# Decay of a gated linear attention: absolute value moved to ScalarE, the stages of two heads set one unit apart

## The chip, the core and the metric

The program runs on one core of a Trainium2 chip. Times are microseconds (us) of device time of one execution of the whole layer. TensorE (PE) does matmuls, ScalarE (ACT) activations and copies, VectorE (DVE) elementwise work and scans, GpSimd (POOL) further elementwise work; SyncE (SP) issues the transfers. Each engine works through its own instructions in order, and one that waits holds up all behind it.

## The reference

One layer of a decoder with two token mixers. After an RMSNorm, one wide projection of h yields everything: queries, keys and values for both mixers, gates, and a rank-16 code for the decay. The change concerns the decay of the gated linear attention, 4 heads of 128 key channels, 1024 tokens, chunks of 64:

```
log_a = jax.nn.log_sigmoid((g_rank @ w_dec_up + b_dec).astype(jnp.float32)) / GLA_TAU      # GLA_TAU = 16
bcum = jnp.cumsum(la, axis=3)                     # within a chunk
qe = qc * jnp.exp(bcum) * (dk ** -0.5)
ke = kc * jnp.exp(-bcum)
```

log_sigmoid(x) is computed as min(x, 0) - ln(1 + exp(-|x|)).

## The kernel before

Every float32 operand is split into a high and a low part (ScalarE copies the high part, VectorE subtracts it: the helper `split`, L161 to L163), and each product is three matmuls. The projection is cut into jobs of 256 columns. A job is a Strassen-like product of 2 by 2 blocks with seven products, called **units** here and numbered through: unit 0 is the first product of job 0, units 7 and 14 are the first of jobs 1 and 2, unit 21 the first of job 3. A unit is 12 matmuls of 128x512 (L267 to L269).

Which unit touches which bank matters (`unit`, L275 to L298). A job has three PSUM banks, x, y and z. Its units 0, 2, 4 and 6 all accumulate into x: so unit 2 may start only when ScalarE has copied what unit 0 left there (`keep`, L273), unit 4 only after the copy behind unit 2, and unit 6 only when VectorE has read x behind unit 4 (`total`, L306).

The operands of coming units are made ready inside the units before (`Pairs.run`): at a job's unit 0 the split of T3 and T4 of the same job, at its units 2, 4 and 6 the splits of the next job's B11/B21 (from the tile raw), T2/T1 (from tt) and B22 (raw to dh, dl). tt holds four differences that GpSimd forms from raw (L241 to L244), for one job at a time: GpSimd starts on the next job when T3 and T4 are split. `run(1, mid)` issues the splits, then the list `mid`, then the unit with its eviction.

The decay of the 4 heads is laid into the first 20 units by such lists, heads 0 and 1 first, then 2 and 3, since the tiles U and E have two buffers each. For head h:

- `logit` (L774): two matmuls (L778) into two banks of the tag tr, of which there are two; VectorE adds the bias from each bank into U (L779).
- `decay_a` (L783): VectorE, E = min(-U, U). `decay_b` (L786): ScalarE, E = exp(E). `decay_c` (L789): ScalarE, E = ln(E + 1).
- `decay_d` (L792): VectorE, E = min(U, 0) - E. `decay_e` (L795): VectorE, the scan along the tokens, into U.
- `decay_f` (L798, L799): ScalarE, E = exp(U/16) and U = exp(-U/16). `decay_g` (L802 to L804): VectorE copies 16 columns out of E; SyncE stores E and U.

The instructions of ScalarE and VectorE stand in these units in the order of the program; PE's are ordered by the scheduler. The chains of heads 2 and 3 are the end of the stage: their last instructions stand in units 16 to 19.

Of the kernel before, what the change touches and what calls it, by code (L numbers as in the profile page):

```python
# [11 lines left out]
AF = mybir.ActivationFunctionType  # L12
ALU = mybir.AluOpType
# [40 lines left out]
class Line:  # L54
# [5 lines left out]
    def run(self, n=None):  # L60
        while self.items and (n is None or n > 0 or not self.items[0][1]):
            f, unit = self.items.pop(0)
            f()
            if unit and n is not None:
                n -= 1


class Pairs:
# [7 lines left out]
        self.at = 0  # L76
        self.first = [j["load"] for j in self.jobs[:2]] + self.jobs[0]["split"][:3]

    def run(self, n=None, mid=()):
        while self.at < 7 * len(self.jobs) and (n is None or n > 0):  # L80
            i, u = divmod(self.at, 7)
            nxt = self.jobs[i + 1] if i + 1 < len(self.jobs) else None
            if u == 0:
                self.jobs[i]["split"][3]()
            elif nxt and u in (2, 4, 6):
                nxt["split"][u // 2 - 1]()
            if u == 1 and i + 2 < len(self.jobs):
                self.jobs[i + 2]["load"]()
            for fn, arg in mid:
                fn(arg)  # L90
            due = self.late.pop(0) if self.late else None
            self.jobs[i]["unit"](u)
            if due:
                due()
            self.at += 1
            if n is not None:
                n -= 1
# [3 lines left out]
def hybrid_layer(ctx: ExitStack, tc: tile.TileContext, x, norm_g, w_in, w_up, b_dec,  # L101
# [5 lines left out]
    nc = tc.nc  # L107
# [421 lines left out]
    def qk_pair(c0, i, dst):  # L529
        def evict(J, n, bank, add):  # L530
            v = total(bank, add)
            o = stage()
            split(v, o[:, 0], o[:, 1])
            nc.sync.dma_start(dst[2 * i + J][:, :, half(n)], o.bitcast(F32))

        return pair_job(w_in, c0 + i * DV, evict)
# [23 lines left out]
    def gg_pair(h):  # L560
        return pair_job(w_in, C_GG + h * DV,
                        lambda J, n, bank, add: silu(total(bank, add), d_gg[h][:, J, half(n)]))

    def merge_pair(c0, i, dst):
        def evict(J, n, bank, add):
            if add is None:
                add = ev.tile([P, HALF], F32, tag="f", name="f")
                nc.scalar.activation(add, bank, AF.Copy)
            else:
                total(bank, add)  # L570
            nc.sync.dma_start(dst[2 * i + J][:, half(n)], add)

        return pair_job(w_in, c0 + i * DV, evict)
# [6 lines left out]
    def sg_pair(i):  # L580

        return pair_job(w_in, C_SG + i * DV,
                        lambda J, n, bank, add: silu(total(bank, add), d_sg[2 * i + J][:, half(n)]))

    def sv_pair(i):


        held = []

        def evict(J, n, bank, add):  # L590
            if add is None:
                add = ev.tile([P, HALF], F32, tag="f", name="f")
                nc.scalar.activation(add, bank, AF.Copy)
            else:
                total(bank, add)
            h = 2 * i + J
            nc.vector.tensor_copy(vend[:, h, 4 * n:4 * n + 4], add[:, P - 1:HALF:P])
            held.append((J, n, h, add))
            if (J, n) != (1, 1):
                while held:  # L600
                    diff(*held.pop())

        def diff(J, n, h, add):
            d = ev.tile([P, HALF], F32, tag="f", name="f")
            nc.vector.tensor_sub(d[:, 1:HALF], add[:, 0:HALF - 1], add[:, 1:HALF])
            if n:
                nc.vector.tensor_sub(d[:, 0:1], vend[:, h, 3:4], add[:, 0:1])
            else:
                nc.vector.tensor_scalar(d[:, 0:1], add[:, 0:1], -1.0, None, op0=ALU.mult)

            def turn():
                pt = ps.tile([P, HALF], F32, tag="tr", name="tr")
                for b in range(4):
                    nc.tensor.transpose(pt[:, b * P:(b + 1) * P], d[:, b * P:(b + 1) * P], ident)
                o = stage()
                split(pt, o[:, 0], o[:, 1])
                for e in range(2):
                    nc.sync.dma_start(d_v[h][:, 4 * n:4 * n + 4, e],
                                      o[:, e].bitcast(F32).rearrange("p (b c) -> p b c", c=P))

            late.append(turn)

        return pair_job(w_in, C_SV + i * DV, evict)

    def gla_qk(i):
        return [gqk_pair(C_GQ, i, inv_sqrt, d_e1, d_gq), gqk_pair(C_GK, i, 1.0, d_e2, d_gk)]

    late = []
    pairs = Pairs([merge_pair(C_MA, i, d_ga) for i in range(3)] +
                  gla_qk(0) + [gg_pair(0), gg_pair(1)] + gla_qk(1) + [gg_pair(2), gg_pair(3)] +  # L630
                  [f for i in range(4) for f in (qk_pair(C_SQ, i, d_q), qk_pair(C_SK, i, d_k))] +
                  [sg_pair(i) for i in range(3)] + [merge_pair(C_MB, i, d_gb) for i in range(4)] +
                  [sv_pair(i) for i in range(4)] + [merge_pair(C_MA, 3, d_ga)], late)
# [132 lines left out]
    U, E = {}, {}  # L766
# [13 lines left out]


    def decay_a(h):
        nc.vector.scalar_tensor_tensor(E[h], U[h], -1.0, U[h], op0=ALU.mult, op1=ALU.min)  # L783

    def decay_b(h):
        nc.scalar.activation(E[h], E[h], AF.Exp)  # L786

    def decay_c(h):
        nc.scalar.activation(E[h], E[h], AF.Ln, bias=1.0)  # L789
# [13 lines left out]
        nc.sync.dma_start(d_e1[h], E[h])  # L803
        nc.sync.dma_start(d_e2[h], U[h])  # L804

    djobs = [[(code, 0)], [(code, 1)]]
    for h in (0, 2):
        djobs += [[(logit, h)], [(logit, h + 1), (decay_a, h)], [(decay_b, h), (decay_a, h + 1)],
                  [(decay_b, h + 1), (decay_c, h)], [(decay_c, h + 1), (decay_d, h), (decay_e, h)],
                  [(decay_d, h + 1), (decay_e, h + 1)], [(decay_f, h)], [(decay_f, h + 1), (decay_g, h)], [(decay_g, h + 1)]]  # L810
    manual = ExitStack()
    manual.enter_context(tc.manual_schedule(engines={mybir.EngineType.Activation, mybir.EngineType.DVE}))
    for jobs in djobs:
        pairs.run(1, jobs)
    dq_ctx.close()


# [22 lines left out]

    tjobs = [[] for _ in range(GLA_AT - len(djobs))]
    for k in range(8):
        at = 4 * k + 3
        for i in range(2):
            tjobs[at + i].append((t_load, (k, i)))
            tjobs[at + 9 + i].append((t_store, (k, i)))
        for i in range(4):
            tjobs[at + 6 + i // 2].append((t_sum, (k, i)))
# [739 lines left out]
```

## Time and profile before

| | before |
|---|---|
| median of 3 runs | 1182.15 us (1180.53 to 1182.76) |
| the profiled execution | 1181.14 us |
| its span, first to last instruction | 1179.4 us |
| PE busy | 1163.8 us, 99% of the span |
| VectorE, ScalarE, GpSimd busy | 861.1, 554.1, 248.2 us |
| decay in the span | from 102.6 us (its first transposes) to 163.1 us (last exponential) |

In a row of a timeline the first number is the start in the span, the second how long the instruction took, then engine, line, operation, output <- inputs, and the shape; x2 means that two in a row are shown as one; in brackets stands how long the engine had been idle before and what ended that.

### The profile page before, as it was taken

The page shows a single profiled execution, that of the slowest core. Times are in us where ns is not written, and L with a number is a line of the kernel's source. Part 1 is how long each engine was busy: PE and PEld are TensorE (multiplying, and loading weights), DVE is VectorE, ACT ScalarE, POOL GpSimd, SP SyncE. Part 2 cuts the span into 40 slices and gives each one's busy share as a digit, 9 for nine tenths or more (in the row PEclk, how much of TensorE's full clock was granted, in tenths as well). Part 3 has the DMA queues.
Part 4 walks back from the last instruction along what each step waited for, and adds up shares of the span by engine and source line. Part 5 has one row for each costly group of instructions (what it writes and reads, how often), then busy time and mean ns, then how long its engine had stood idle before and what let it go on. Part 6 is the DMA issues. An engine that isn't in the chain of part 4 may idle for free.

```text
span 1179.4 us, 16601 instructions
## 1 busy us (share of the span) xinstructions
PE 1163.8 (99%) x5811; PEld 978.4 (83%) x5811; DVE 861.1 (73%) x1440; ACT 554.1 (47%) x1040; POOL 248.2 (21%) x217
## 2 busy tenths in 40 slices
PE   8999999999999999999999999999999999999997
PEld 8999778888888888888888888888888888888886
DVE  6797866887676876776666677457777876588986
ACT  6555652433545544545444343344454544364543
POOL 1022341324242242342242232000000000700001
PEclk9999999999999999999999999999999999999999
DMA  7325469897355565654444357799756556858652
GB/s 289 126 63 161 173 233 320 294 308 242 123 189 185 186 221 165 196 179 136 154 144 132 109 173 240 258 310 333 258 188 226 194 166 196 281 162 286 212 197 107
DMA packets 189455, 239.23 MB, mean 203 GB/s; under 512 B 12438, under 2 KB 128172, under 8 KB 187836
## 3 DMA queue, kind: packets, MB, share of 16 engines
q1 hardware_dynamic: 188796, 237.13, 60.9%
q8 instruction: 45, 0.74, 0.3%
q10 hardware_dynamic: 576, 1.05, 0.2%
q14 instruction: 38, 0.31, 0.1%
HBM read 150.06 MB, written 88.08 MB: 202 GB/s over the span
## 4 chain that ended last, share of the span: by engine, by line
PE 89%; DVE 4%; ACT 2%; issue 2%; DMA 2%; POOL 1%; SPq 0%; ACTq 0%; DVEq 0%
PE pp L267 16%; PE pp L269 16%; PE pp L268 16%; PE pp L203 3%; PE pp L202 3%; PE pp L201 3%; PE pp L220 2%; PE tr L1083 1%; PE av L1106 1%; PE av L1105 1%; PE av L1104 1%; PE z L1065 1%; PE z L1067 1%; PE z L1066 1%; PE xb L1472 1%
## 5 line engine op out<-in xcount | busy, mean ns | idle before, releaser
L267 PE MATMUL pp<-S,wh 128*128 128x512 f32 x372 | 147.2, 396 | 1.0 <-ACT f L273 1.0
L269 PE MATMUL pp<-S,wl 128*128 128x512 f32 x372 | 145.0, 390 | 0.0
L268 PE MATMUL pp<-S,wh 128*128 128x512 f32 x372 | 145.0, 390 | 0.0
L306 DVE TENSOR_TENSOR f<-pp,f 128x512 f32<-128x512 f32 x93 | 63.9, 687 | 76.0 <-PE pp L269 65.0
L163 DVE TENSOR_TENSOR wl<-tt,wh 128x1024 fp32r<-128x1024 f32 x62 | 75.9, 1224 | 51.5 <-ACT wh L162 51.1
L162 ACT ACTIVATE wh<-tt 128x1024 fp32r<-128x1024 f32 x62 | 65.7, 1059 | 74.8 <-PE pp L268 67.3
L241 POOL TENSOR_TENSOR tt<-raw 128x512 f32<-128x512 f32 x31 | 44.4, 1432 | 258.3 <-DVE wl L163 250.5
L273 ACT ACTIVATE f<-pp 128x512 f32<-128x512 f32 x93 | 54.9, 592 | 88.1 <-PE pp L269 84.8
L1071 DVE TENSOR_TENSOR_SCAN be<-be,m 128x128 f32<-128x128 f32 (+3 forms) x64 | 86.1, 1348 | 6.9 <-ACT be L1068 6.7
L162 ACT ACTIVATE wh<-raw 128x1024 fp32r<-128x1024 f32 (+1 forms) x47 | 48.4, 1031 | 85.9 <-PE pp L268 51.5
L267 PEld LDWEIGHTS pp<-S,wh 128*128 128x128 f32 x372 | 70.5, 190 | 15.9 <-ACT f L273 1.8
L269 PEld LDWEIGHTS pp<-S,wl 128*128 128x128 f32 x372 | 69.8, 188 | 14.9
L268 PEld LDWEIGHTS pp<-S,wh 128*128 128x128 f32 x372 | 69.9, 188 | 13.7
L163 DVE TENSOR_TENSOR wl<-raw,wh 128x1024 fp32r<-128x1024 f32 (+1 forms) x47 | 63.8, 1357 | 15.8 <-ACT wh L162 15.2
L228 POOL TENSOR_TENSOR r<-r,nhalf 128x1 f32<-128x1 f32 x40 | 25.2, 629 | 194.5 <-DVE r L227 194.5
L1068 ACT ACTIVATE be<-z 128x384 f32<-128x384 f32 (+4 forms) x96 | 47.2, 495 | 22.5 <-PE z L1067 20.0
L1255 POOL TENSOR_TENSOR N<-A,A 128x512 f32<-128x512 f32 x4 | 5.7, 1424 | 242.1 <-DMA A<-d_osb 242.1
L267 PE MATMUL pp<-ha22h,wh 128*128 128x512 f32 x124 | 48.8, 394 | 0.7 <-DVE f L306 0.7
L267 PE MATMUL pp<-ha11h,wh 128*128 128x512 f32 x124 | 49.2, 397 | 0.0
L267 PE MATMUL pp<-ha12h,wh 128*128 128x512 f32 x124 | 49.1, 396 | 0.0
L267 PE MATMUL pp<-S,dh 128*128 128x512 f32 x124 | 48.6, 392 | 0.0
L244 POOL TENSOR_TENSOR tt<-raw,tt 128x512 f32<-128x512 f32 x31 | 48.0, 1549 | 2.2
(528 smaller groups left out, 3398.4 us busy)
## 6 DMA issues: line engine op xcount, KB each, us to landing
raw<-in_w_in_dram SPq DMA_DIRECT2D x31, 1024.0 KB, 5.8
d_t<-t SPq DMA_DIRECT2D x16, 512.0 KB, 6.6
d_ogl<-o SPq DMA_DIRECT2D x64, 128.0 KB, 2.5
d_q<-o SPq DMA_DIRECT2D x16, 512.0 KB, 3.2
d_k<-o SPq DMA_DIRECT2D x16, 512.0 KB, 4.8
d_v<-o SPq DMA_DIRECT2D x32, 256.0 KB, 2.3
k<-d_k SPq DMA_DIRECT2D x8, 1024.0 KB, 6.1
v<-d_v SPq DMA_DIRECT2D x16, 512.0 KB, 5.1
```

What stands on the lines that cost most here:

```text
L162: nc.scalar.activation(hi, src, AF.Copy)
L163: eng.tensor_sub(lo, src, hi.bitcast(F32))
L201: nc.tensor.matmul(pt, whi[:, kb], h_, start=kb == 0, stop=False)
L241: nc.gpsimd.tensor_sub(t1, b[:, 0, 1], b[:, 0, 0])
L244: nc.gpsimd.tensor_sub(t4, b[:, 1, 0], t2)
L267: nc.tensor.matmul(pt, bh[:, j], ah[:, j], start=first and j == 0, stop=False, skip_group_check=True)
L268: nc.tensor.matmul(pt, bh[:, j], al[:, j], start=False, stop=False, skip_group_check=True)
L269: nc.tensor.matmul(pt, bl[:, j], ah[:, j], start=False, stop=j == 3, skip_group_check=True)
L273: nc.scalar.activation(t[nm], t[bank], AF.Copy)
L306: nc.vector.tensor_add(add, bank, add)
L1068: nc.scalar.activation(om[:, off + pc * w:off + (pc + 1) * w], zt[:, 0:w], AF.Sigmoid, scale=-inv_sqrt)
L1071: nc.vector.tensor_tensor_scan(rest, rest, m1[:, off:T][:, ::-1], 1.0, op0=ALU.mult, op1=ALU.max)
```

## The change

`decay_a` becomes an activation Abs on ScalarE, and `decay_b` gets the factor -1. `Pairs.run` gets a second list, `post`, that is issued behind the unit and its eviction; `decay_f` goes there. Of the two heads of a pair, the second now has its scan (`decay_e`) one unit behind its `decay_d`. Heads 2 and 3 begin at unit 10 in place of 11, so that the decay takes 19 units and not 20; the lists that follow are shifted by one entry to stay at the same units.

```
-    def run(self, n=None, mid=()):
+    def run(self, n=None, mid=(), post=()):
...
             self.jobs[i]["unit"](u)
+            for fn, arg in post:
+                fn(arg)
...
     def decay_a(h):
-        nc.vector.scalar_tensor_tensor(E[h], U[h], -1.0, U[h], op0=ALU.mult, op1=ALU.min)
+        nc.scalar.activation(E[h], U[h], AF.Abs)
 
     def decay_b(h):
-        nc.scalar.activation(E[h], E[h], AF.Exp)
+        nc.scalar.activation(E[h], E[h], AF.Exp, scale=-1.0)
...
-    djobs = [[(code, 0)], [(code, 1)]]
-    for h in (0, 2):
-        djobs += [[(logit, h)], [(logit, h + 1), (decay_a, h)], [(decay_b, h), (decay_a, h + 1)],
-                  [(decay_b, h + 1), (decay_c, h)], [(decay_c, h + 1), (decay_d, h), (decay_e, h)],
-                  [(decay_d, h + 1), (decay_e, h + 1)], [(decay_f, h)], [(decay_f, h + 1), (decay_g, h)], [(decay_g, h + 1)]]
+    djobs = [([(code, 0)], []), ([(code, 1)], [])] + [([], []) for _ in range(17)]
+    for h, at in ((0, 2), (2, 10)):
+        for i, fn, h_ in ((0, logit, h), (1, logit, h + 1), (1, decay_a, h), (2, decay_b, h), (2, decay_a, h + 1),
+                          (3, decay_b, h + 1), (3, decay_c, h), (4, decay_c, h + 1), (4, decay_d, h), (4, decay_e, h),
+                          (5, decay_d, h + 1), (6, decay_e, h + 1), (7, decay_g, h), (8, decay_g, h + 1)):
+            djobs[at + i][0].append((fn, h_))
+        for i, h_ in ((6, h), (7, h + 1)):
+            djobs[at + i][1].append((decay_f, h_))
...
-        pairs.run(1, jobs)
+        pairs.run(1, *jobs)
...
-        at = 4 * k + 3
+        at = 4 * k + 4
```

Line numbers after the change are two higher up to the decay, and a few more behind it (L162 is L164, L273 is L275, L778 is L780, L786 is L788, L789 is L791, L798 and L799 are L800 and L801).

Three places show what this moves. The first is PE where the logits of head 3 are computed. Before, its two matmuls stand inside unit 12 (the products with dh and dl; S_1004 and S_1005 are the high and low part of S4), with three others between them:

```order
L269 MATMUL pp<-S_1080,wl 128x512
L267 MATMUL pp<-S_1004,dh 128x512
L268 MATMUL pp<-S_1005,dh 128x512
L778 MATMUL tr<-rst,o 128x512
L269 MATMUL pp<-S_1004,dl 128x512
L267 MATMUL pp<-S_1004,dh 128x512
L268 MATMUL pp<-S_1005,dh 128x512
L778 MATMUL tr<-rst,o 128x512
```

Now both stand together between unit 10 (with S_807 and S_808, the parts of S1) and unit 11 (S_1080 and S_1081, of S3):

```order
L269 MATMUL pp<-S_807,wh 128x512
L270 MATMUL pp<-S_808,wh 128x512
L271 MATMUL pp<-S_807,wl 128x512
L780 MATMUL tr<-rst,o 128x512 x2
L269 MATMUL pp<-S_1080,wh 128x512
L270 MATMUL pp<-S_1081,wh 128x512
```

Head 2's pair stands in front of unit 10, where before it stood in front of unit 11: between it and the first matmul of head 3 lay 14 matmuls, and now lie 12. On VectorE head 2's two bias additions now follow directly on the copies of head 1's `decay_g`, where a split of tt stood between.

The second place is ScalarE around unit 13, in heads 2 and 3. Before, from the split of B22 (dh) on: one exponential, the eviction of unit 13 (L568), the split of T3 and T4 (wh from tt), the other exponential, a table load, the logarithms:

```order
L162 ACTIVATE dh<-raw 128x512
L786 ACTIVATE e<-e 128x1024
L568 ACTIVATE f<-pp 128x512
L162 ACTIVATE wh<-tt 128x1024
L786 ACTIVATE e<-e 128x1024
L789 ACT_TABLE_LOAD
L789 ACTIVATE e<-e 128x1024
L273 ACTIVATE f<-pp 128x512
```

Now the exponential, the table load and the first logarithm stand ahead of that eviction and that split:

```order
L164 ACTIVATE dh<-raw 128x512
L788 ACTIVATE e<-e 128x1024
L791 ACT_TABLE_LOAD
L791 ACTIVATE e<-e 128x1024
L570 ACTIVATE f<-pp 128x512
L164 ACTIVATE wh<-tt 128x1024
L791 ACTIVATE e<-e 128x1024
L275 ACTIVATE f<-pp 128x512
```

The third place is ScalarE around units 17 and 18. Before, from the last table load: head 2's two exponentials, the copy behind unit 17, the split of tt for unit 18 (T2 and T1 of job 3), then head 3's two exponentials:

```order
L798 ACT_TABLE_LOAD
L798 ACTIVATE e<-u 128x1024
L799 ACTIVATE u<-u 128x1024
L273 ACTIVATE f<-pp 128x512
L162 ACTIVATE wh<-tt 128x1024
L798 ACTIVATE e<-u 128x1024
L799 ACTIVATE u<-u 128x1024
L162 ACTIVATE dh<-raw 128x512
```

Now head 3's exponentials, as the list behind unit 17, stand ahead of that split:

```order
L800 ACT_TABLE_LOAD
L800 ACTIVATE e<-u 128x1024
L801 ACTIVATE u<-u 128x1024
L275 ACTIVATE f<-pp 128x512
L800 ACTIVATE e<-u 128x1024
L801 ACTIVATE u<-u 128x1024
L164 ACTIVATE wh<-tt 128x1024
L164 ACTIVATE dh<-raw 128x512
```

On VectorE the lower part of that split is followed, before and now, by one small copy of `decay_g` (head 2's before, head 3's now) and then by the reading of bank x behind unit 18. The number of table loads in the stage is four in both. Behind the decay no engine's order changes.

## The prediction

> **What bounds the kernel now.** I read the page's head first, then the waits of PE in the stretch of the decay (102 to 166 us), then the timelines of PE, VectorE, ScalarE and GpSimd there.
>
> ```profile
> span 1179.4 us, 16601 instructions
> PE 1163.8 (99%) x5811; PEld 978.4 (83%) x5811; DVE 861.1 (73%) x1440; ACT 554.1 (47%) x1040; POOL 248.2 (21%) x217
> PE pp L267 <- ACT f L273: 1.0, 1, 1.0
> PE pp L267 <- DVE f L306: 0.7, 1, 0.7
> PE tr L778 <- DVE u L779: 0.3, 1, 0.3
> ```
>
> PE is busy 99% of the span, so the end moves only by what PE waits. An engine with time to spare gains nothing from less work; it counts only where PE waits for it. In the decay these are three waits, 2.0 us together. Their exact size, with a fourth, is in PE's timeline: each row before a wait, and the row behind it.
>
> ```profile
> 134.36 0.61 PE L778 MATMUL tr<-rst,o 128*128 128x512 f32 x2
> 135.97 0.50 PE L267 MATMUL pp<-S,wh 128*128 128x512 f32 x1 [1.00 <-ACT f L273]
> 139.05 0.39 PE L268 MATMUL pp<-S,dh 128*128 128x512 f32 x1
> 139.73 0.50 PE L778 MATMUL tr<-rst,o 128*128 128x512 f32 x1 [0.29 <-DVE u L779]
> 150.53 0.39 PE L269 MATMUL pp<-ha12h,wl 128*128 128x512 f32 x1
> 150.91 0.50 PE L267 MATMUL pp<-S,wh 128*128 128x512 f32 x1
> 161.70 0.39 PE L269 MATMUL pp<-S,dl 128*128 128x512 f32 x1
> 162.80 0.50 PE L267 MATMUL pp<-ha22h,wh 128*128 128x512 f32 x1 [0.72 <-DVE f L306]
> ```
>
> A matmul starts every 0.227 us (the two at 134.36 take 0.61 together, one alone 0.39). So unit 11 should have started at 134.81 and came at 135.97, 1.16 late; the logit of head 3 came 0.45 late, unit 16 0.15, unit 20 0.87. Each first matmul after a wait takes 0.50 in place of 0.39, 0.11 more. Sum: 2.63 + 0.44 = 3.07 us, 0.26% of the time. That is all the change can win, unless it makes the rest of the program quicker, and behind the decay the order is the same.
>
> **The parts that cost nothing by themselves.** VectorE loses four L783 (1.2 us each), ScalarE gets four Abs. Abs isn't in this trace. The nearest row is an activation of the same shape:
>
> ```profile
> 119.49 1.06 ACT L786 ACTIVATE e<-e 128x1024 f32<-128x1024 f32 x1 [1.48 <-DVE e L783]
> ```
>
> I take its 1.06, with 0.60 (half the shape, the eviction at 145.51 below) and 1.3 (a table load, at 148.02 below) as ends. The order shows the same four table loads, so none is added. PE waits for no Abs directly. The exponential of head 1 waited 1.48 here for VectorE's L783; now Abs takes 1.06 of ScalarE in that place, so the chain of heads 0 and 1 comes some 0.4 earlier. The factor -1 in the exponential changes no shape. The stores of E and U keep their places in SyncE's queue, but for the very last one, which now goes ahead of one store of gate logits; the next to need them is unit 21. I set all this at 0, ends -0.4 and +0.5.
>
> **Head 3's logits now wait for VectorE (+0.9).** VectorE and GpSimd in the stretch where heads 0 and 1 end:
>
> ```profile
> 129.98 3.27 DVE L795 TENSOR_TENSOR_SCAN u<-rmask,e 128x1024 f32<-128x1024 f32 x1
> 133.17 0.66 DVE L306 TENSOR_TENSOR f<-pp,f 128x512 f32<-128x512 f32 x1
> 133.76 1.68 DVE L163 TENSOR_TENSOR wl<-raw,wh 128x1024 fp32r<-128x1024 f32 x1
> 135.35 1.32 DVE L802 COPY ebl<-e 128x16 f32<-128x16 f32 x2
> 138.94 1.40 DVE L779 TENSOR_SCALAR u<-tr,vcol 128x512 f32<-128x512 f32 x2
> 131.06 3.28 POOL L243 TENSOR_TENSOR tt<-raw 128x512 f32<-128x512 f32 x1
> 134.31 2.25 POOL L242 TENSOR_TENSOR tt<-raw,tt 128x512 f32<-128x512 f32 x1
> 136.64 1.30 POOL L244 TENSOR_TENSOR tt<-raw,tt 128x512 f32<-128x512 f32 x1
> ```
>
> See how they exclude each other. The scan takes 3.27, where 2.29 is its time alone (a row below). GpSimd's L243 takes 3.28, where L244 at 136.64 takes 1.30: it waits for the scan's end at 133.25. The split at 133.76 takes 1.68 and not 1.23: it waits for L243's end at 134.34. The copies of heads 0 and 1 start at 135.35 and end at 136.67, just behind L242 (136.56). Only the work on PSUM (L306, L779) goes on beside. I call this the lock. Up to these copies VectorE's order is unchanged, so they end at about 136.4 (the 0.4 from above, less a little). Then head 2's bias additions follow: 0.7 each, to 137.1 and 137.8.
>
> PE is there earlier. Unit 10 began at 134.36 less its 12 x 0.227, at 131.64. Now head 2's two matmuls and unit 10 stand there, 14 x 0.227, so head 3's first matmul is due at 134.82. It needs the first tr bank, free at 137.1: 2.3 late, and the second 0.26 more. With the slow restart 2.7 us, where before the first two waits cost 1.16 + 0.11 + 0.45 + 0.11 = 1.83. The wait of unit 11 for ScalarE's copy goes, since that copy now stands ahead of head 1's exponentials; but it is replaced by a longer one. Net +0.9. The wait at unit 16 goes (-0.26): PE comes there 1 us later, and the copy it needs does not.
>
> **Unit 20 now waits behind head 3's exponentials (+4.4).** ScalarE and VectorE at the end of the decay:
>
> ```profile
> 142.57 0.63 ACT L162 ACTIVATE dh<-raw 128x512 fp32r<-128x512 f32 x1 [4.91 <-PE pp L268]
> 145.51 0.60 ACT L568 ACTIVATE f<-pp 128x512 f32<-128x512 f32 x1 [1.03 <-PE pp L269]
> 146.01 1.05 ACT L162 ACTIVATE wh<-tt 128x1024 fp32r<-128x1024 f32 x1
> 148.02 1.28 ACT L789 ACT_TABLE_LOAD   x1
> 158.41 1.05 ACT L162 ACTIVATE wh<-tt 128x1024 fp32r<-128x1024 f32 x1
> 160.98 1.06 ACT L798 ACTIVATE e<-u 128x1024 f32<-128x1024 f32 x1 [1.52 <-DVE u L795]
> 147.09 1.23 DVE L163 TENSOR_TENSOR wl<-tt,wh 128x1024 fp32r<-128x1024 f32 x1 [1.37 <-ACT wh L162]
> 150.41 1.61 DVE L792 SCALAR_TENSOR_TENSOR e<-u,e 128x1024 f32<-128x1024 f32 x1 [2.09 <-ACT e L789]
> 152.05 3.27 DVE L795 TENSOR_TENSOR_SCAN u<-rmask,e 128x1024 f32<-128x1024 f32 x1
> 155.82 1.67 DVE L163 TENSOR_TENSOR wl<-raw,wh 128x1024 fp32r<-128x1024 f32 x1
> 158.66 2.29 DVE L795 TENSOR_TENSOR_SCAN u<-rmask,e 128x1024 f32<-128x1024 f32 x1
> 162.07 0.68 DVE L306 TENSOR_TENSOR f<-pp,f 128x512 f32<-128x512 f32 x1
> ```
>
> Unit 20 needs the reading of bank x at 162.07. In VectorE's queue that stands behind the split whose upper part is ScalarE's row at 158.41. That row came before head 3's exponentials (160.98, which waited for the scan). Now it comes behind both. Step by step, from unit 11: it starts 2.7 us behind 134.82 + 0.45, at 138.0, and two units of 2.72 bring unit 13 to 143.5:
>
> - dh can start when unit 12 is done, 143.7. Then 0.49 for it, 0.96 exponential, 1.29 table load, 0.96 logarithm, 0.49 eviction, 0.96 split (rows that follow each other lie 0.1 closer than they last): the split of T3 and T4 is done at 149.0, on VectorE at 150.15, where it was at 148.3.
> - From there to the end of the second scan VectorE has 1.13 (L792) + 2.2 (scan) + 1.13 (L792) + 1.13 (split) + 2.2 (scan) = 7.8 under the lock, and GpSimd, which starts behind the same split, its four differences of 1.2. Before, two of these four ran while VectorE waited for the logarithm (150.41); now there is no such gap, and they alternate. Sum 12.6, end at 162.8. Before, it was 160.95.
> - Head 3's exponentials 2.2, the split 1.06, its lower part 1.2, a copy 0.1, the reading 0.7, with the signals between: 168.1.
> - PE: unit 13 at 143.5, seven units of 2.72 and one matmul that is drawn ahead: due at 162.8. So it waits 5.3, and 0.11 for the restart, where 0.98 stood: +4.4.
>
> What else would hold PE in that gap? Nothing is queued for it: the rest of the order is behind this unit.
>
> **The clock after such a gap (+2.4).** After the waits in the rows above, of 1.2 us or less, only the first matmul was slow. Longer stretches without PE are only at the two ends:
>
> ```profile
> 1.42 5.91 PE L146 MATMUL warm<-ident 128*128 128x128 f32 x26 [1.42 <-POOL ident masks.py:199]
> 8.52 1.06 PE L146 MATMUL warm<-ident 128*128 128x128 f32 x8
> 1172.50:1174.50 2.00, 0.00 (x0) 0.00 (x0) 1.56 (x3) 1.26 (x3) 0.21 (x1) 1.00 0.43 165
> 1174.50:1175.00 0.50, 0.00 (x0) 0.00 (x0) 0.13 (x1) 0.08 (x2) 0.34 (x1) 0.90 0.55 217
> 1175.00:1179.40 4.40, 0.00 (x0) 0.00 (x0) 0.62 (x1) 0.71 (x1) 0.00 (x0) 0.50 0.56 214
> ```
>
> After the last matmul the granted clock (the column ahead of the last two) falls to 0.50 within 2.4 us. At the start the same 128x128 matmul takes 5.91 / 26 = 0.23 us each, and from 8.52 on 0.13: PE ran slow for some 6 to 7 us of steady work. So a gap of 5.3 us should end with the clock at half, and PE should need between half of that time and all of it to come back: 3.3 to 6.6 us at half speed, 1.6 to 3.3 lost. I take 2.4, with 0 (no drop) as the other end. [...]
>
> **Sum.** 0.9 - 0.26 + 4.4 + 2.4 = +7.4. Against the profiled execution (1181.14, of which 1.7 lie outside the span) that is 1188.5; the median of the three runs is 1.0 higher than this execution, which would give 1189.5. I say 1189.0.
>
> **The rivals.**
> - *The clock stays up.* The same waits, no slow stretch: 1181.6 (between the two bases) + 5.0 = 1186.6. Against it stands the tail; for it, that the tail is one case, and that PE's clock is seen to fall nowhere else. [...]
> - *The lock does not bite.* Were GpSimd's differences out of the way, the copies would end at 133.5 and both tr banks be free by 134.9: no wait there. The second scan would end at 155.9, unit 20 be due at 160.0 and have its bank at 161.4: 1.5 + 0.11 in place of 3.07, 1180.1. Against it: the stretched rows above; GpSimd starts on the same splits as before.
> - *The change does what its parts say, and the waits go: faster.* For it: the copy for unit 11 does stand ahead of the exponentials now, and heads 2 and 3 begin a unit earlier. If VectorE had head 2's additions done by 134.8 and head 3's scan ended at 157.6, 5.2 us ahead of what I say, all four waits would go: 3.07 less, 1178.5. That is the point that decides; the scan ended at 160.95 before, and the work ahead of it has only moved together.
> - *The second wait is milder.* If GpSimd loses two turns to VectorE, the scan ends 2.4 earlier and no clock falls: +2.6, 1184.2.
> - *Both gaps cool PE.* The first, 2.6 us in all, is near the tail's 2.4: another 1.6 to 2.4, 1191.
>
> **Chances and range.** Forecast 0.56; clock stays 0.17; lock does not bite 0.08; waits go 0.07; milder 0.07; both gaps 0.05. A measurement of this kernel can tell about 0.2% from no change, 2.4 us: faster is below 1179.8, slower above 1184.5. Faster: the case of the waits and a little of the lock's, 0.08. Same: the rest of the lock's and a small part of the milder, 0.09. Slower 0.83. The range from 1183.5 to 1192.0 leaves out the waits' and the lock's case and a little above.
>
> **What will show it.** In the profile after: PE's waits in the decay are two: the second logit pair (L780) for VectorE's L781, 2 to 2.6 us, at about 135; and unit 20 (ha22h) for VectorE's L308, 4.5 to 5.5 us, at about 163. The wait for ScalarE's copy (L275) is gone. ScalarE's split of tt follows head 3's exponentials directly. Behind 168 the granted clock shows a slow stretch of 3 to 7 us. I am wrong if unit 20 waits under 2 us, if the second scan ends ahead of 160, or if PE waits somewhere else for longer.

## The result and the profile after

The kernel after takes 1188.01 us (median of 6 runs, 1185.47 to 1188.6), before 1180.83 (6 runs, 1179.89 to 1182.76): ratio 1.0054, 95% interval 1.0044 to 1.0065. It is slower by some 7 us; the forecast was 1189.0. The profiled execution took 1187.92 us with a span of 1186.2, 6.8 more than before.

PE's waits from 102 to 175 us, to set beside the three waits of before:

```profile
PE pp L269 <- DVE f L308: 4.5, 1, 4.5
PE tr L780 <- DVE u L781: 2.1, 2, 1.9
```

The wait for ScalarE's copy is gone. The two waits for VectorE, 0.7 and 0.3 before, have grown, at the two places that the prediction named. The timeline of PE has the rows around both:

```profile
134.62 0.39 PE L271 MATMUL pp<-S,wl 128*128 128x512 f32 x1
136.92 0.50 PE L780 MATMUL tr<-rst,o 128*128 128x512 f32 x1 [1.91 <-DVE u L781]
137.57 0.50 PE L780 MATMUL tr<-rst,o 128*128 128x512 f32 x1 [0.15 <-DVE u L781]
...
164.04 0.39 PE L269 MATMUL pp<-ha11h,wh 128*128 128x512 f32 x1
168.89 0.80 PE L269 MATMUL pp<-ha22h,wh 128*128 128x512 f32 x1 [4.46 <-DVE f L308]
...
169.91 0.63 PE L271 MATMUL pp<-ha22h,wl 128*128 128x512 f32 x1
170.33 0.63 PE L269 MATMUL pp<-ha22h,wh 128*128 128x512 f32 x1
```

Head 3's logits came 2.07 and 0.42 us late (136.92 less 134.62 + 0.227, and so on), unit 20 came 4.62 late. The last two rows show a matmul every 0.42 us in place of 0.227; it was so behind both gaps. The windows there show why. A row gives a stretch and its length, then the busy time of PE, of its weight loads, of VectorE, ScalarE and GpSimd with their instructions in brackets; the granted clock is the column ahead of the last two:

```profile
134.70:138.10 3.40, 1.33 (x5) 0.67 (x4) 3.40 (x6) 2.48 (x4) 2.67 (x2) 1.00 0.81 330
138.20:141.40 3.20, 3.20 (x9) 2.53 (x8) 1.77 (x3) 2.53 (x3) 0.00 (x0) 0.50 0.00 0
165.40:168.80 3.40, 0.00 (x0) 0.00 (x0) 1.88 (x4) 2.01 (x3) 0.00 (x0) 1.00 0.75 308
169.00:172.20 3.20, 3.20 (x8) 2.52 (x9) 1.03 (x2) 0.00 (x0) 0.00 (x0) 0.50 0.69 205
```

The granted clock fell to half behind both gaps, not only behind the second. The slow matmuls lost 1.56 us at the first (8 times 0.195) and 1.65 at the second. Summed over the stretch, PE is 10.4 us late where it was 3.07 late before: +7.4, against +6.8 in the span. The other 0.6 comes back far behind the decay: a transpose at 706.84 us of before starts 7.40 later in after, one at 914.67 only 6.86 later, as before waits 0.47 and 0.67 for VectorE between 912 and 915 us and after, there, 0.52 once.

The causes stand in the other engines' timelines. VectorE and GpSimd, with the rows of the prediction's steps:

```profile
133.29 1.67 DVE L165 TENSOR_TENSOR wl<-raw,wh 128x1024 fp32r<-128x1024 f32 x1
134.89 1.31 DVE L804 COPY ebl<-e 128x16 f32<-128x16 f32 x2
136.12 1.39 DVE L781 TENSOR_SCALAR u<-tr,vcol 128x512 f32<-128x512 f32 x2
150.39 1.22 DVE L165 TENSOR_TENSOR wl<-tt,wh 128x1024 fp32r<-128x1024 f32 x1 [3.90 <-ACT wh L164]
152.79 3.27 DVE L797 TENSOR_TENSOR_SCAN u<-rmask,e 128x1024 f32<-128x1024 f32 x1
155.98 2.24 DVE L794 SCALAR_TENSOR_TENSOR e<-u,e 128x1024 f32<-128x1024 f32 x1
158.75 1.72 DVE L165 TENSOR_TENSOR wl<-raw,wh 128x1024 fp32r<-128x1024 f32 x1
160.39 3.37 DVE L797 TENSOR_TENSOR_SCAN u<-rmask,e 128x1024 f32<-128x1024 f32 x1
166.92 1.23 DVE L165 TENSOR_TENSOR wl<-tt,wh 128x1024 fp32r<-128x1024 f32 x1 [3.09 <-ACT wh L164]
168.15 1.28 DVE L308 TENSOR_TENSOR f<-pp,f 128x512 f32<-128x512 f32 x2
133.84 2.25 POOL L244 TENSOR_TENSOR tt<-raw,tt 128x512 f32<-128x512 f32 x1
153.87 3.27 POOL L245 TENSOR_TENSOR tt<-raw 128x512 f32<-128x512 f32 x1
159.46 2.16 POOL L246 TENSOR_TENSOR tt<-raw,tt 128x512 f32<-128x512 f32 x1
```

At 134.89 the two copies of 16 columns take 1.31 together, to 136.20, just behind GpSimd's L244 (133.84 to 136.09); only then come head 2's additions. From 150.39 on, VectorE and GpSimd alternate: scans of 3.27 and 3.37, an L794 of 2.24, until 163.76. ScalarE:

```profile
144.97 0.63 ACT L164 ACTIVATE dh<-raw 128x512 fp32r<-128x512 f32 x1 [3.91 <-PE pp L270]
163.79 1.06 ACT L800 ACTIVATE e<-u 128x1024 f32<-128x1024 f32 x1 [3.17 <-DVE u L797]
164.88 1.06 ACT L801 ACTIVATE u<-u 128x1024 f32<-128x1024 f32 x1
165.85 1.04 ACT L164 ACTIVATE wh<-tt 128x1024 fp32r<-128x1024 f32 x1
```

The split at 165.85 stands behind head 3's two exponentials; VectorE's lower part (166.92), its reading of bank x (168.15) and unit 20 (168.89) follow one upon the other.

### The profile page after: what moved, and what is told of

It is laid out like the page before. It is cut to its first block, busy times and chain, and to the rows that moved or that the text cites. A ratio compares the mean times of both kernels' runs of the same rounds, so it can differ in the third digit from the quotient of the medians.

```text
span 1186.2 us, 16600 instructions
## 1 busy us (share of the span) xinstructions
PE 1165.6 (98%) x5811; PEld 979.9 (83%) x5811; DVE 857.4 (72%) x1436; ACT 558.6 (47%) x1044; POOL 250.2 (21%) x217
## 4 chain that ended last, share of the span: by engine, by line
PE 88%; DVE 4%; DMA 3%; ACT 2%; issue 2%; SPq 0%; ACTq 0%; DVEq 0%
PE pp L269 16%; PE pp L270 16%; PE pp L271 16%; PE pp L204 3%; PE pp L203 3%; PE pp L205 3%; PE pp L222 2%; PE av L1111 1%; PE av L1110 1%; PE av L1109 1%; PE tr L1088 1%; PE xb L1477 1%; PE xb L1475 1%; PE xb L1476 1%; PE z L1070 1%
## 5 line engine op out<-in xcount | busy, mean ns | idle before, releaser
L164 ACT ACTIVATE wh<-tt 128x1024 fp32r<-128x1024 f32 x62 | 65.6, 1058 | 75.1 <-PE pp L270 67.3
L275 ACT ACTIVATE f<-pp 128x512 f32<-128x512 f32 x93 | 55.1, 593 | 87.8 <-PE pp L271 80.4
L164 ACT ACTIVATE wh<-raw 128x1024 fp32r<-128x1024 f32 (+1 forms) x47 | 48.5, 1031 | 86.2 <-PE pp L270 50.9
L270 PE MATMUL pp<-ha22l,wh 128*128 128x512 f32 x124 | 48.9, 394 | 0.0
L271 PE MATMUL pp<-ha22h,wl 128*128 128x512 f32 x124 | 48.8, 394 | 0.0
```

The source lines that it names most:

```text
L164: nc.scalar.activation(hi, src, AF.Copy)
L270: nc.tensor.matmul(pt, bh[:, j], al[:, j], start=False, stop=False, skip_group_check=True)
L271: nc.tensor.matmul(pt, bl[:, j], ah[:, j], start=False, stop=j == 3, skip_group_check=True)
L275: nc.scalar.activation(t[nm], t[bank], AF.Copy)
```

## The experiments

All were timed in five rounds beside before, whose median was 1180.77 to 1181.22 us in each set. The theory: two gaps and the clock behind each are the whole loss; the first comes from the lock on the copies, the second from head 3's exponentials ahead of the split, with the lock on the way to them. The rivals: Abs costs; the spread costs wherever it stands; the lock is no cause; the slow stretches do not come from the gaps.

**Abs alone.** Before, with two lines changed:

```
-        nc.vector.scalar_tensor_tensor(E[h], U[h], -1.0, U[h], op0=ALU.mult, op1=ALU.min)
+        nc.scalar.activation(E[h], U[h], AF.Abs)
...
-        nc.scalar.activation(E[h], E[h], AF.Exp)
+        nc.scalar.activation(E[h], E[h], AF.Exp, scale=-1.0)
```

> The kernel before with only the absolute value on ScalarE (Abs, then exp with the factor -1); order of the stages as before. My theory, that Abs itself costs nothing and the loss lies in where the stages stand: the time of before, -0.5 to +0.3 us, the wait of unit 11 a little shorter than 1.16, the wait of unit 20 about 0.9 as before, no slow clock. Rival, that four more activations on ScalarE are what delays the copies and splits: +1 us or more, with PE waits on ScalarE's rows.

1180.15 us, ratio 0.9995 (0.9986 to 1.0003). The rows of an Abs and of unit 11's first matmul:

```profile
139.88 1.06 ACT L783 ACTIVATE e<-u 128x1024 f32<-128x1024 f32 x1 [2.72 <-DVE u L779]
135.48 0.50 PE L267 MATMUL pp<-S,wh 128*128 128x512 f32 x1 [0.52 <-ACT f L273]
```

An Abs takes 1.06. Unit 11 came 0.68 late in place of 1.16. The Abs costs nothing.

**The spread alone.** After, with these lines put back as in before (the minimum on VectorE).

> The changed kernel with the absolute value back on VectorE, all else as changed. Theory (the order of the stages is the loss): as slow as the changed kernel, +6.5 to +8 us over before, both waits there (logits of head 3 about 2 to 2.6, unit 20 about 4.5 to 5.5) and the clock at half behind each. Rival (Abs is the loss): within 2 us of before.

1189.65 us, ratio 1.0071 (1.0058 to 1.0084): both waits (2.56 and 0.43 late, 4.63 late), both slow stretches. The order makes the loss.

**Head 3's exponentials behind the split.** After, with one of the four pairs placed elsewhere:

```
-            djobs[at + i][1].append((decay_f, h_))
+            if h_ == 3:
+                djobs[18][0].insert(0, (decay_f, h_))
+            else:
+                djobs[at + i][1].append((decay_f, h_))
```

> The changed kernel with head 3's two exponentials moved behind the split of T2 and T1 at unit 18, where they stood before; nothing else is moved. Theory (unit 20 waits because that split stands behind them): the split is done before the second scan ends, the wait of unit 20 falls from 4.5 to about 1 to 2.4, and with it the slow clock behind it; the wait for head 3's logits (about 2) and the slow clock behind it stay. Time +2.5 to +4 over before. Rival (the second scan itself, late by GpSimd's lock, holds the reading of bank x): the wait stays over 4 and the time at +6 or more.

1183.65 us, ratio 1.0021 (1.0012 to 1.0029). PE's timeline has one row that matters, against 4.46 in after:

```profile
167.13 0.50 PE L269 MATMUL pp<-ha22h,wh 128*128 128x512 f32 x1 [1.52 <-DVE f L308]
```

Unit 20 waits 1.52, and behind it the matmuls come at full pace (the next at 167.48). The first gap and its slow stretch are as in after. So the place of head 3's exponentials was worth 4.4 of the 7 us.

**Without GpSimd's differences of job 3.** After, where tt is only set to a constant for that job, so that the kernel leaves out a part of the result:

```
+            if not sums:
+                nc.gpsimd.memset(tt, 0.5)
+                t["b"], t["tt"] = b, tt
+                return
...
-        return pair_job(w_in, c0 + i * DV, evict, before)
+        return pair_job(w_in, c0 + i * DV, evict, before, sums=(c0, i) != (C_GQ, 0))
```

> After without GpSimd's four differences for job 3: a memset of tt stands in their place, so that job's part of the projection (the gated attention's queries of heads 0 and 1) is not computed from the input. Theory (GpSimd and VectorE exclude each other; the differences stretch VectorE's way to head 3's scan): L794, scan, L794, split, scan run at their own lengths, the second scan ends near 159.5 in place of 163.7, and unit 20 waits about 1.7 us in place of 4.6 and its clock stays up behind it; the first gap behind head 3's logits is unchanged (the differences of job 2 stand there). Time about 1.1 + 1.6 us above before, some 1183.5. Rival (the scan is late because of ScalarE's order, the lock is no cause): unit 20 waits over 4 us as in after, time as after.

1183.4 us, ratio 1.002 (1.0011 to 1.0029). VectorE's and GpSimd's timelines, to set beside the rows from 150 on above (the line numbers of the decay are four higher here):

```profile
152.69 2.29 DVE L801 TENSOR_TENSOR_SCAN u<-rmask,e 128x1024 f32<-128x1024 f32 x1
154.89 1.20 DVE L798 SCALAR_TENSOR_TENSOR e<-u,e 128x1024 f32<-128x1024 f32 x1
156.61 1.22 DVE L165 TENSOR_TENSOR wl<-raw,wh 128x1024 fp32r<-128x1024 f32 x1
157.74 2.29 DVE L801 TENSOR_TENSOR_SCAN u<-rmask,e 128x1024 f32<-128x1024 f32 x1
151.57 1.81 POOL L244 MEMSET tt<- 128x2048 f32 x1 [14.21 <-DVE wl L165]
```

All instructions have their own lengths, the second scan ends at 160.0 and not 163.8, and unit 20 comes 1.33 late in place of 4.62, with the clock up. ScalarE's order is that of after. So the second wait has two causes that make it long only together, the lock and the place of head 3's exponentials: with either one taken away it is under 2 us.

**Spare matmuls in the gap.** After, with work for PE ahead of unit 20 that nothing reads:

```
+        if pairs.at == 20:
+            fill = ps.tile([P, HALF], F32, tag="av", name="fill", bufs=1)
+            for _ in range(16):
+                nc.tensor.matmul(fill, ident, kept_f[C_MA, 2, 0, 0], start=True, stop=True)
```

> The changed kernel with 16 more matmuls of 128x512 into an unused bank ahead of unit 20 (they read a tile that has long been written, and nothing reads the bank). They take 16 x 0.227 = 3.6 us of a gap of 4.6. Theory (the gap lets the clock fall, which costs 1.6 us in slow matmuls): unit 20 starts at the same time, its matmuls come every 0.227 and not 0.43, and the time is 1.3 to 1.7 us below the changed kernel. Rival (the slow matmuls behind the gap have another cause, such as operands or banks): they stay slow and the time is that of the changed kernel or more.

1196.97 us, ratio 1.014 (1.0126 to 1.0155). The expectation was wrong by the price of a matmul: on float32 operands one took 0.83 us, not 0.227 (16 from 164.04 to 177.38), and they overshot the gap by 8.5 us. With five in place of sixteen (the profile shows each as two rows):

> After with five spare matmuls of 128x512 (float32, identity times the value tile, into a bank of their own that nothing reads) ahead of unit 20. In the run with sixteen they took about 0.83 us each, so five take some 4.2 us of the 4.85 us in which PE stands there otherwise. Theory (the gap itself cools PE, by 1.6 us): unit 20 starts at the time it starts in after (168.9), behind it the matmuls come every 0.23 us and not 0.43, and the kernel takes 1.3 to 1.7 us less than after, about 1186.5. Rival (the slow stretch belongs to the units behind, or to the time of the run, not to the gap): the stretch stays and the time is that of after, or longer by what the spare matmuls overshoot.

1186.71 us (1186.2 to 1186.99), ratio 1.005 (1.0037 to 1.0062). PE's timeline:

```profile
163.93 4.46 PE L862 MATMUL fill<-f,ident 128*128 128x512 f32 x10
168.76 0.50 PE L269 MATMUL pp<-ha22h,wh 128*128 128x512 f32 x1 [0.37 <-DVE f L308]
169.09 0.39 PE L270 MATMUL pp<-ha22l,wh 128*128 128x512 f32 x1
```

Unit 20 starts at the same time as in after (168.89), but no slow stretch follows. The median lies 1.3 us below after's, the size expected. The intervals of the two ratios overlap, so the time alone would not show it; the rows do. The granted clock is 1.00 from 168.60 to 172.00 here, where in after it is 0.50 from 169.00 to 172.20: in this kernel the empty gap, and not the units behind it, is what lowers the clock.

**The first gap.** After, with head 1's copy of 16 columns put behind head 2's additions:

```
+            if (fn, h_) == (decay_g, 1):
+                last = (fn, h_)
+                continue
             djobs[at + i][0].append((fn, h_))
+            if (fn, h_) == (logit, 2):
+                djobs[at + i][0].append(last)
```

> After with one thing moved: head 1's copy of 16 columns (and the issue of its two stores) stands behind head 2's two bias additions and no longer ahead of them. Theory (head 3's logits wait only because VectorE's locked copies stand ahead of the additions that free the two tr banks): the first bank comes free one copy, 0.66 us, earlier, PE's first gap shrinks from 2.07 + 0.42 to about 1.4 + 0.4, so that the clock stays up behind it (gaps of 1.7 us and less did not lower it in the other runs, one of 2.1 did); unit 20 moves with it and still waits about 4.5, with its slow stretch. Time 0.6 + 1.6 us below after, near 1186. Rival (the additions wait for PE's own logits or for the split ahead of the copies): the gap and the time stay as in after.

A miss: 1188.53 us, ratio 1.0067 (1.0053 to 1.008), as after. VectorE's timeline says why:

```profile
134.78 1.23 DVE L804 COPY ebl<-e 128x16 f32<-128x16 f32 x1
135.93 1.40 DVE L781 TENSOR_SCALAR u<-tr,vcol 128x512 f32<-128x512 f32 x2
137.25 0.16 DVE L804 COPY ebl<-e 128x16 f32<-128x16 f32 x1
```

I had halved the 1.31 us of the two copies. But a copy alone takes 0.16; the first takes the whole wait for GpSimd, whichever it is. So all four copies went to ScalarE, together with the remedy for the second gap:

```
-        nc.vector.tensor_copy(ebl[:, h], ch3(E[h])[:, :, CH - 1])
+        nc.scalar.activation(ebl[:, h], ch3(E[h])[:, :, CH - 1], AF.Copy)
```

> After with two remedies: head 3's exponentials ahead of unit 18 but behind its split (as in the version that took 1183.65), and the four copies of 16 columns on ScalarE in place of VectorE. In the version with head 1's copy moved, that copy took 0.16 us alone, and head 0's, left where it was, took the whole wait for GpSimd's difference of 2.2 us; so what costs is not the copies' length but that any locked instruction stands there. Theory (two gaps and the clock behind each are the whole loss; the first is the lock on the copies): without a copy there, head 2's additions on PSUM start when the split ends, at 135.0 in place of 136.1; the first gap shrinks from 2.07 + 0.43 to about 0.9 + 0.4 us, the second stays near 1.7, and the clock falls behind neither. Near 1180.9, as before, although heads 2 and 3 begin at unit 10. Rivals: the additions wait for something else, first gap and its slow stretch stay, 1183.6; or something further in the spread costs, 1183 or more with both gaps small.

1181.01 us, ratio 1.0005 (0.9996 to 1.0014): before's time, with heads 2 and 3 begun at unit 10 and the stages spread. VectorE's timeline:

```profile
133.22 1.67 DVE L165 TENSOR_TENSOR wl<-raw,wh 128x1024 fp32r<-128x1024 f32 x1
134.81 1.40 DVE L781 TENSOR_SCALAR u<-tr,vcol 128x512 f32<-128x512 f32 x2
```

The additions follow the split at once. Head 3's logits come 0.82 and 0.43 late, unit 20 1.50, and no stretch is slow. Against the kernel with the second remedy alone the copies were worth 2.6 us. Nothing further in the spread costs.

**Another place.** After, with heads 2 and 3 begun later, and the lists behind shifted to stay at their units; for unit 13:

```
-    djobs = [([(code, 0)], []), ([(code, 1)], [])] + [([], []) for _ in range(17)]
-    for h, at in ((0, 2), (2, 10)):
+    djobs = [([(code, 0)], []), ([(code, 1)], [])] + [([], []) for _ in range(20)]
+    for h, at in ((0, 2), (2, 13)):
...
-        at = 4 * k + 4
+        at = 4 * k + 1
```

> After with heads 2 and 3 begun at unit 11 in place of 10, where before has them. Theory: head 3's logits wait about 1.3 us and unit 20 about 1.8 us, neither enough to lower the clock; the time equals before within 0.5 us, so that the whole loss of the change is the one unit by which heads 2 and 3 were advanced. Rival (the spread stages cost by themselves): 2 us or more above before.

> After with heads 2 and 3 begun at unit 12 in place of 10. Theory: head 3's logits come without a wait, as the copies of heads 0 and 1 are done; unit 20 waits about 1.8 us for the reading of its bank behind head 3's work, too little for the clock to fall, and the time is about 1 to 1.5 us below before, near 1179.5. Rival (the spread costs by itself): above before, with a slow stretch of the clock.

> After with heads 2 and 3 begun at unit 13 in place of 10 (the spread of the stages and the exponentials behind the eviction are kept; the lists that follow are shifted to stay at their units). Theory (both losses come from where these stages meet the splits, the copies of heads 0 and 1 and the differences of a job's change): head 3's logits find both banks free, head 3's scan and exponentials now stand in units 19 and 20, behind the split that unit 18 and 20 need, so that PE waits under 0.5 us in the whole decay and no slow stretch is seen; about 1.5 to 3.4 us below before, 1177.5 to 1179.5. Rival (spreading the stages one unit apart costs by itself, wherever it stands): waits of 2 us and more elsewhere, and a time above before.

| heads 2 and 3 from | time, us | ratio to before (95%) | late in the profiled execution, us: logits, unit 20 |
|---|---|---|---|
| unit 10 (after) | 1188.01 | 1.0054 (1.0044 to 1.0065) | 2.07 + 0.42, 4.62 |
| unit 11 | 1180.87 | 0.9998 (0.999 to 1.0007) | 1.26, 1.55 |
| unit 12 | 1179.53 | 0.9994 (0.9985 to 1.0003) | none, 1.87 |
| unit 13 | 1178.31 | 0.9978 (0.9969 to 0.9986) | none, none |

One unit decides: where before has these heads, the spread costs nothing, and from unit 13 PE has no wait in the decay at all and the kernel is 2.5 us quicker than before. That version beats both. Is it the place or the spread? Before, with only the place changed:

```
     for h in (0, 2):
+        djobs += [[], []] if h else []
...
-        at = 4 * k + 3
+        at = 4 * k + 1
```

> Before, with nothing changed but that heads 2 and 3 begin at unit 13 in place of 11 (the minimum on VectorE, the stages together, the exponentials ahead of the unit, as in before). It tells what of the gain of the version with the spread stages at unit 13 is place alone. Theory (the waits come from where the stages meet the change of job): most of before's 3.1 us goes here too, as head 3's last stages are over behind unit 20; what stays is the wait for ScalarE's copy behind unit 9 (about 1 us), since head 1's exponentials stand ahead of that copy as in before. About 1179. Rival (the spread is what removes the waits): 1181 or more, with waits of 2 us and above at units 18 to 21.

The theory fell here: 1183.72 us, ratio 1.0023 (1.0013 to 1.0032), slower than before. Unit 20 waits again, 2.01 late, and unit 11 comes 1.62 late for ScalarE's copy. The profiled execution is the quickest of the ten, 1181.59, and has no slow stretch between units; the others have mean clocks of 0.998 to 0.996 where it has 0.999. VectorE's timeline of this kernel and then of the spread stages at unit 13:

```profile
160.40 1.22 DVE L792 SCALAR_TENSOR_TENSOR e<-u,e 128x1024 f32<-128x1024 f32 x1
161.66 2.29 DVE L795 TENSOR_TENSOR_SCAN u<-rmask,e 128x1024 f32<-128x1024 f32 x1
163.86 1.26 DVE L306 TENSOR_TENSOR f<-pp,f 128x512 f32<-128x512 f32 x2
```

```profile
157.80 1.22 DVE L794 SCALAR_TENSOR_TENSOR e<-u,e 128x1024 f32<-128x1024 f32 x1
158.94 0.68 DVE L308 TENSOR_TENSOR f<-pp,f 128x512 f32<-128x512 f32 x1
159.54 2.28 DVE L797 TENSOR_TENSOR_SCAN u<-rmask,e 128x1024 f32<-128x1024 f32 x1
```

Together, head 3's L792 and scan both stand ahead of the reading that unit 20 needs; one unit apart, the reading slips in between. Unit 11's wait has another cause: ScalarE's copy stands behind head 1's exponentials there, as in before, and ahead of them in the order of the change. So at unit 13 the order of the change gains 5.4 us over the old one, and at unit 10 it met the wrong neighbours. How much of the 5.4 is the spread, how much the exponentials behind the unit and how much the Abs wasn't tried apart, and the old order begun at unit 10 was not run.

## Why the prediction was right, point by point

- *What bounds the kernel; the parts that cost nothing.* Right: Abs 1.06 as taken, and no difference from it alone. The wait that this relieves (unit 11's for ScalarE's copy) was 0.48 shorter.
- *Head 3's logits, +0.9.* Right in mechanism and size: copies done at 136.20 (forecast 136.4), logits 2.07 and 0.42 late (forecast 2.3 and 0.26) with 0.11 for the restart, 2.6 in place of 2.7; the wait at unit 16 went. The version with the copies on ScalarE shows the cause.
- *Unit 20, +4.4.* Right in mechanism: 4.62 late and not 5.3, so +3.75. Both ends moved. The chain began 1.3 later (dh at 144.97, forecast 143.7), because PE ran slow behind the first gap; from the split's end (151.6) to the second scan's end VectorE took 12.1, forecast 12.6; the reading was done at 168.85, forecast 168.1. PE was due at 164.27, forecast 162.8. So PE's delay took more of the wait away than the chain's delay gave back.
- *The clock, +2.4.* Here a step failed: one drop was counted, and there were two. "Both gaps cool PE" had a chance of 0.05, though its own sentence had the argument: a first gap of 2.6 us in all is near the 2.4 in which the tail's clock fell. The tail was one draw besides: from the end of the last matmul to the fall it is 2.4 us in before and 3.3 in after. The size of one drop was too high too: 1.56 and 1.65 were lost, at the lower end of 1.6 to 3.3. Two of 1.6 are 3.2, where 2.4 was said.
- *The sum.* 0.8 (logits) - 0.26 + 3.75 + 3.2 = 7.5, forecast 7.4. That it fits so well is luck: the second wait was 0.65 too long and the clock 0.8 too cheap.
- *The rivals.* The clock did not stay up; the lock does bite (the run without the differences); the waits that go are to be had, but from unit 13 on.

## What to carry to other kernels

A chain that is laid beside a full PE costs by what it stands next to, not by its length: moving it by one unit was worth 7 us, and the spread order was slower than the kernel before at one place and quicker at another. Before moving a stage, list what each queue it enters already holds there, and whether the next engine's instruction contends with another engine's. A gap of PE of some 2 us cost nearly double here where a slow stretch followed it: behind the 2.07 us of after's first gap another 1.56 were lost, behind the 4.62 of its second 1.65, and behind the 2.01 of before's order from unit 13 nothing in its profiled execution.

## What the runs showed of the hardware

The clock. Behind a gap between units, each slow stretch whose clock was read lasted 3.4 us at a granted clock of 0.50; the two of after cost 1.56 and 1.65 us. Two narrow windows of after show where its stretches begin:

```profile
138.00:138.20 0.20, 0.20 (x3) 0.16 (x2) 0.20 (x1) 0.20 (x1) 0.00 (x0) 0.86 0.00 0
168.80:169.00 0.20, 0.11 (x1) 0.12 (x1) 0.20 (x2) 0.00 (x0) 0.00 (x0) 0.66 0.00 0
```

A mean of 0.86 is half speed for the last 28% of the window, so from 138.14; 0.66 is half speed from 168.86. They lie 30.7 us apart, nine times 3.41. In the spread alone (139.31 and 170.02) and in the copy behind the additions (138.56 and 169.28) the two lie 30.7 us apart as well. In the kernel with head 3's exponentials behind the split, one slow stretch begins at 13.29 and the next at 139.59, 126.30 us apart, 37 times 3.41. So it looks as if a clock of 3.41 us ran on by itself, and PE's speed changed only on its beat; that is my estimate from these starts and lengths.

What decides on a beat is open. In the windows of after PE was busy 1.33 of the 3.40 us ahead of the first fall (39%) and 0.00 ahead of the second. But the share of busy time in that stretch sets no boundary, as one execution of the spread alone shows, with two stretches on the beat and what followed each:

```profile
135.89:139.31 3.42, 1.81 (x7) 1.27 (x8) 3.42 (x6) 1.06 (x2) 1.90 (x2) 1.00 0.57 231
139.31:142.72 3.41, 3.41 (x10) 2.65 (x9) 2.22 (x3) 1.06 (x1) 0.00 (x0) 0.50 0.00 0
163.20:166.61 3.41, 1.67 (x8) 1.05 (x6) 1.08 (x2) 2.33 (x3) 0.00 (x0) 1.00 0.15 60
166.61:170.02 3.41, 0.68 (x3) 0.58 (x4) 2.65 (x5) 1.25 (x2) 0.00 (x0) 1.00 0.61 251
```

Busy 53% ahead of a fall, and 49% ahead of none. The length of a gap sorts the profiled executions better, though not cleanly. Between units, gaps of 1.71 us without work or less (the longest in the kernel with the heads from unit 12) had no slow stretch behind them, and all of 1.89 or more had one. Of the two between, 1.83 (the copy behind the additions) had one and 1.85 (before's order from unit 13) had none. Each of these is a single execution.

A beat that runs by itself would also make runs of one kernel differ, as the same gap falls differently on it; their mean clocks fit that, though no run was made to show it. After's quickest run, 1185.47 us, has a mean clock of 0.998, its slowest, 1188.6, 0.995; the version of before from unit 13, with a gap of 2.01 us, goes from 1181.59 (0.999) to 1185.62 (0.996). PE's start differs too: the profiled execution of the kernel with the heads from unit 12, 1181.46 us against a median of 1179.53, has a slow stretch at 13.4 us (granted clock 0.50 from 13.40 to 16.60), which that of after has not (1.00 there).

The lock. A copy of 16 columns, 0.16 us long, stood 1.23 us for a difference on GpSimd; an addition from PSUM in its place started at once (at 134.81, against 136.12 in after).
